# Average pooling over 64 x 256 rows: the store of a run issued by a landing signal, and one run summed by tensor_reduce

## The chip, the core and the metric

The kernel runs on one core of a Trainium2 chip. The time is device microseconds of that core for one execution, and less is better. A core has several engines that run their own instruction streams and meet through semaphores; here SyncE (SP) issues loads, VectorE (DVE) adds, ScalarE (ACT) multiplies and issues stores. All transfers are carried out by the same 16 DMA engines, whichever engine issues them. Each issuing engine has a DMA queue of its own: q1 holds what SyncE issues, q10 what ScalarE issues.

## The reference

The input is 64 x 256 x 8192 float32 numbers (537 MB). Kernel size and stride are both 4, so every output element is the mean of four neighbours that no other output uses; the output has 64 x 256 x 2048 numbers (134 MB).

```python
out_len = (length - kernel_size) // stride + 1
for i in range(out_len):
    start = i * stride
    output[:, :, i] = np.mean(x[:, :, start : start + kernel_size], axis=2)
```

## The kernel before

The input is seen as one long row and cut into 64 blocks of 128 partitions x 16384 elements (8.39 MB each, 64 KB in a partition). Two blocks make a run, so there are 32 runs, numbered 0 to 31; n is the run, k (0 or 1) the block within it. A run's output is 128 x 8192 elements (4.19 MB, 32 KB in a partition) and leaves in one store.

There are two input buffers, xt0 for the first and xt1 for the second block of every run, and two output buffers, ot0 and ot1, used in turn by even and odd runs (q in the code).

All order is written out by hand with semaphores. The helper `take` (L59) waits until a semaphore has reached a number and takes this number off again. `pair` (L82) issues the instructions of one run on all engines:

- VectorE takes `full[k]`, which block k's load counts up when it has landed; for the first block it also takes `stored[q]`, which the store out of the same output buffer, two runs earlier, counts up. Then `sums` (L74) adds neighbours: L76 adds even and odd elements into the first half of the block's own buffer, a drain follows, and L78 adds even and odd elements of that half into the output buffer.
- The end of L78 counts up `free`. SyncE takes it, counts up `summed` for ScalarE, and issues the next run's load of the same k into the buffer that came free (L63, through the argument `ahead`).
- ScalarE takes `summed` and multiplies the block's sums by a quarter in place (L94).
- After the second block, the engine given as `store` takes `scaled` and issues the run's store (L98). It is ScalarE for runs 0 to 29 and SyncE for run 30.

Runs 0 to 29 are in a loop of 15 passes with two runs each. Run 30 follows outside the loop (L123); its `ahead` loads the first block of run 31 whole and the second in two halves of columns (L114), each with a semaphore of its own. Run 31 is written out: VectorE sums the first block, then each half of the second; ScalarE multiplies, and stores in two parts (L142): 3 MB with the first half, the last 1 MB with the second. SyncE at last waits for all stores.

At the start, the loads of run 0 are issued (L70), and a small ScalarE instruction (L102) and an increment mark the two output buffers as free.

Of the kernel before, what the change touches and what calls it, by code (L numbers as in the profile page):

```python
# [1 line left out]

# [4 lines left out]


FULL = 16384
PAIR = 2  # L10
ROUND = 2 * PAIR

TAIL = (8192, 8192)


@with_exitstack
def kernel(
    ctx: ExitStack,
    tc: tile.TileContext,
    x: bass.AP,  # L20
    kernel_size: bass.AP,
    stride: bass.AP,
    out: bass.AP,
):
    nc = tc.nc
    K, S = int(kernel_size), int(stride)
    assert K == S == 4
    B, C, L = x.shape
    assert L % K == 0
    P = nc.NUM_PARTITIONS  # L30
    dt = x.dtype
    add, mult = mybir.AluOpType.add, mybir.AluOpType.mult

    M = FULL // K
    blocks = B * C * L // P // FULL
    runs = blocks // PAIR
    assert blocks * P * FULL == B * C * L and blocks % ROUND == 0 and sum(TAIL) == FULL

    xr = x.rearrange("b c l -> (b c l)").rearrange("(n p k m) -> n k p m", p=P, k=PAIR, m=FULL)
    orun = out.rearrange("b c l -> (b c l)").rearrange("(n p m) -> n p m", p=P, m=PAIR * M)  # L40


    xt0 = ctx.enter_context(nc.sbuf_tensor([P, FULL], dt))
    xt1 = ctx.enter_context(nc.sbuf_tensor([P, FULL], dt))
    ot0 = ctx.enter_context(nc.sbuf_tensor([P, PAIR * M], dt))
    ot1 = ctx.enter_context(nc.sbuf_tensor([P, PAIR * M], dt))
    xt, ot = [xt0, xt1], [ot0, ot1]


    full = [nc.alloc_semaphore(f"full{k}") for k in range(2)]  # L50
    piece = [nc.alloc_semaphore(f"piece{k}") for k in range(len(TAIL))]
    free = nc.alloc_semaphore("free")
    summed = nc.alloc_semaphore("summed")
    summed_last = nc.alloc_semaphore("summed_last")
    scaled = nc.alloc_semaphore("scaled")
    scaled_last = nc.alloc_semaphore("scaled_last")
    stored = [nc.alloc_semaphore(f"stored{k}") for k in range(2)]

    def take(engine, sem, n):  # L59
        engine.wait_ge(sem, n).then_inc(sem, -n)  # L60

    def load(n, k):
        d = nc.sync.dma_start(out=xt[k][:, :], in_=xr[n, k])  # L63
        d.then_inc(full[k], 16)
        return d

    for k in range(2):
        tc.no_tile_sem_insts.add(load(0, k).ins.name)  # L70
    tc.close()
    tc.compile()  # L72

    def sums(t, o):  # L74
        w = t.shape[1]
        nc.vector.tensor_tensor(out=t[:, : w // 2], in0=t[:, ::2], in1=t[:, 1::2], op=add)  # L76
        nc.vector.drain()
        return nc.vector.tensor_tensor(  # L78
            out=o, in0=t[:, : w // 2 : 2], in1=t[:, 1 : w // 2 : 2], op=add
        )  # L80

    def pair(n, q, ahead, store):  # L82

        for k in range(PAIR):
            take(nc.vector, full[k], 16)
            if k == 0:
                take(nc.vector, stored[q], 16)
            sums(xt[k][:, :], ot[q][:, k * M : (k + 1) * M]).then_inc(free, 1)
            take(nc.sync, free, 1)
            nc.sync.sem_inc(summed, 1)  # L90
            ahead(k)
            o = ot[q][:, k * M : (k + 1) * M]
            take(nc.scalar, summed, 1)
            means = nc.scalar.mul(o, o, 1.0 / K)  # L94
        done = scaled if store is nc.scalar else scaled_last
        means.then_inc(done, 1)
        take(store, done, 1)
        store.dma_start(out=orun[n], in_=ot[q][:, :]).then_inc(stored[q], 16)  # L98


    zero = nc.const_aps.tensor(0.0, [P, 1], dt)
    nc.scalar.mul(ot[0][:, :1], zero, 1.0).then_inc(stored[0], 16)  # L102
    nc.scalar.sem_inc(stored[1], 16)

    edges = [sum(TAIL[:i]) for i in range(len(TAIL) + 1)]
    pieces = list(zip(edges[:-1], edges[1:]))
    xe, oe = xr[runs - 1, 1], orun[runs - 1]

    def ahead_of_last(k):
        if k == 0:  # L110
            load(runs - 1, 0)
        else:
            for sem, (a, b) in zip(piece, pieces):
                nc.sync.dma_start(out=xt[1][:, a:b], in_=xe[:, a:b]).then_inc(sem, 16)  # L114

    engines = (mybir.EngineType.SP, mybir.EngineType.DVE, mybir.EngineType.Activation)
    with nc.Fori(0, (runs - 2) // 2, 1, engines=engines) as r:
        for q in range(2):
            n = r * 2 + q
            pair(n, q, lambda k: load(n + 1, k), nc.scalar)  # L120


    pair(runs - 2, 0, ahead_of_last, nc.sync)  # L123

    take(nc.vector, stored[1], 16)
    take(nc.vector, full[0], 16)
    sums(xt[0][:, :], ot[1][:, :M]).then_inc(summed_last, 1)
    for k, (sem, (a, b)) in enumerate(zip(piece, pieces)):  # L130
        take(nc.vector, sem, 16)
        sums(xt[1][:, a:b], ot[1][:, M + a // K : M + b // K]).then_inc(summed_last, 1)
        if k == 0:
            take(nc.scalar, summed_last, 1)
            nc.scalar.mul(ot[1][:, :M], ot[1][:, :M], 1.0 / K)  # L135
        o = ot[1][:, M + a // K : M + b // K]
        take(nc.scalar, summed_last, 1)
        nc.scalar.mul(o, o, 1.0 / K).then_inc(scaled, 1)  # L138
        take(nc.scalar, scaled, 1)
        c = 0 if k == 0 else M + a // K  # L140
        d = M + b // K
        nc.scalar.dma_start(out=oe[:, c:d], in_=ot[1][:, c:d]).then_inc(stored[1], 16)  # L142
    take(nc.sync, stored[0], 16)
    take(nc.sync, stored[1], 16 * len(TAIL))


# [1 line left out]
_INS = ['x', 'kernel_size', 'stride']  # L148
_OUTS = [((64, 256, 2048), 'float32')]

_NUMBERS = {'kernel_size': 4, 'stride': 4}


# [26 lines left out]
```

## Time and profile before

| | us |
|---|---|
| median of 3 runs | 1578.83 |
| lowest, highest | 1573.74, 1585.71 |
| the profiled execution, its own time | 1578.58 |
| its span in the profile | 1577.3 |
| L76 over 128 x 8192 results, mean of one | 8.692 |
| L78 over 128 x 4096 results, mean of one | 4.425 |
| L94 over 128 x 4096, mean of one | 3.616 |
| VectorE idle in front of L76, in total | 720.1 |
| ScalarE idle in front of L94, in total | 1307.6 |

The profile is of one execution. Its page lists busy time by engine and by line, the share of the span in which the 16 DMA engines moved data, in 40 equal slices and by queue, and the DMA issues with the time from issue to landing. The trace behind it answers finer questions: a timeline of instructions with the idle time before each, and busy time and bytes in any stretch. Issuing a DMA and waiting on a semaphore do not count as busy time. The trace also has a record of every packet that the DMA engines moved, with its queue, size, start and duration; a packet here is one partition's row of a block. Times in the text are microseconds from the start of the span.

### The profile page before, as it was taken

The page shows a single profiled execution, that of the slowest core. Times are in us where ns is not written, and L with a number is a line of the kernel's source. Part 1 is how long each engine was busy: PE and PEld are TensorE (multiplying, and loading weights), DVE is VectorE, ACT ScalarE, POOL GpSimd, SP SyncE. Part 2 cuts the span into 40 slices and gives each one's busy share as a digit, 9 for nine tenths or more (in the row PEclk, how much of TensorE's full clock was granted, in tenths as well). Part 3 has the DMA queues.
Part 4 walks back from the last instruction along what each step waited for, and adds up shares of the span by engine and source line. Part 5 has one row for each costly group of instructions (what it writes and reads, how often), then busy time and mean ns, then how long its engine had stood idle before and what let it go on. Part 6 is the DMA issues. An engine that isn't in the chain of part 4 may idle for free. (4 is left out here: it accounts for less than half of the span.)

```text
span 1577.3 us, 1028 instructions
## 1 busy us (share of the span) xinstructions
DVE 839.8 (53%) x130; ACT 233.1 (15%) x67; POOL 0.2 (0%) x4
## 2 busy tenths in 40 slices
DVE  3654546545465454654546545465454654546546
ACT  1101011010110101101011010110101101011011
POOL 0000000000000000000000000000000000000000
DMA  9999999999999999999999999999999999999999
GB/s 425 425 425 425 435 439 420 430 434 430 420 427 419 445 420 427 420 420 444 425 425 412 425 438 424 422 415 425 437 425 427 414 421 441 417 430 420 416 435 388
DMA packets 14112, 671.09 MB, mean 425 GB/s; under 512 B 1568, under 2 KB 1568, under 8 KB 1568
## 3 DMA queue, kind: packets, MB, share of 16 engines
q1 hardware_dynamic: 9504, 541.07, 80.7%
q10 hardware_dynamic: 4608, 130.03, 19.1%
HBM read 536.87 MB, written 134.22 MB: 425 GB/s over the span
## 5 line engine op out<-in xcount | busy, mean ns | idle before, releaser
L76 DVE TENSOR_TENSOR xt<-xt 128x8192 f32<-128x8192 f32 (+1 forms) x65 | 556.5, 8561 | 720.1 <-DVEq L60 720.1
L94 ACT ACTIVATE ot<-ot 128x4096 f32<-128x4096 f32 x62 | 224.2, 3616 | 1307.6 <-ACTq L60 1307.6
L78 DVE TENSOR_TENSOR ot<-xt 128x4096 f32<-128x4096 f32 (+1 forms) x65 | 283.4, 4360 | 4.8
L135 ACT ACTIVATE ot<-ot 128x4096 f32<-128x4096 f32 x1 | 3.6, 3617 | 15.6 <-ACTq L60 15.6
L138 ACT ACTIVATE ot<-ot 128x2048 f32<-128x2048 f32 x2 | 3.8, 1910 | 8.0 <-ACTq L60 8.0
L102 ACT ACT_TABLE_LOAD x1 | 1.3, 1283 | 2.4 <-PEq L72 2.4
L102 ACT ACTIVATE ot<-const-float32-0.0 128x1 f32<-128x1 f32 x1 | 0.2, 203 | 0.0
L161 POOL MEMSET const-bfloat16-1.0<- 128x1 bf16 x1 | 0.1, 102 | 0.0
L161 POOL MEMSET const-uint8-127<- 128x1 uint8 x1 | 0.1, 102 | 0.0
L161 POOL MEMSET const-float32-1.0<- 128x1 f32 x1 | 0.1, 99 | 0.0
L161 POOL MEMSET const-float32-0.0<- 128x1 f32 x1 | 0.1, 98 | 0.2 <-issue 0.2
## 6 DMA issues: line engine op xcount, KB each, us to landing
out_dram<-ot ACTq DMA_DIRECT2D x30, 4096.0 KB, 33.8
xt<-in_x_dram SPq DMA_DIRECT2D x2, 4096.0 KB, 20.5
out_dram<-ot SPq DMA_DIRECT2D x1, 4096.0 KB, 34.4
out_dram<-ot ACTq DMA_DIRECT2D x1, 3072.0 KB, 13.8
out_dram<-ot ACTq DMA_DIRECT2D x1, 1024.0 KB, 10.4
xt<-in_x_dram SPq DMA_DIRECT2D x63, 35.6
```

The lines of the kernel that those rows point to most:

```text
L76: nc.vector.tensor_tensor(out=t[:, : w // 2], in0=t[:, ::2], in1=t[:, 1::2], op=add)
L78: return nc.vector.tensor_tensor(out=o, in0=t[:, : w // 2 : 2], in1=t[:, 1 : w // 2 : 2], op=add)
L94: means = nc.scalar.mul(o, o, 1.0 / K)
L102: nc.scalar.mul(ot[0][:, :1], zero, 1.0).then_inc(stored[0], 16)
L135: nc.scalar.mul(ot[1][:, :M], ot[1][:, :M], 1.0 / K)
L138: nc.scalar.mul(o, o, 1.0 / K).then_inc(scaled, 1)
L161: nc = _bacc.Bacc("TRN2", target_bir_lowering=False, num_devices=1)
```

## The change

ScalarE's store gets one more wait. A new semaphore, `landed`, is counted up by VectorE whenever it has taken `full[0]`, that is, when the first block of a run has landed, before it begins its sums. ScalarE takes one count of it ahead of issuing a run's store. Since run 0's own first block also counts it up, ScalarE takes one count at the start, so that the store of run n waits for the first block of run n + 1. This holds for runs 0 to 29. The store of run 30, which SyncE issues, and those of run 31 don't wait for it.

In run 30, both blocks are summed by a new function, `reduce`: one `tensor_reduce` over groups of four neighbours, from the input buffer to the output buffer, in place of the two additions and the drain. All other runs keep `sums`.

```diff
+    landed = nc.alloc_semaphore("landed")
...
+    def reduce(t, o):
+        return nc.vector.tensor_reduce(
+            out=o,
+            in_=t.rearrange("p (m k) -> p m k", k=K),
+            op=add,
+            axis=mybir.AxisListType.X,
+        )
+
     def pair(n, q, ahead, store):
         for k in range(PAIR):
             take(nc.vector, full[k], 16)
             if k == 0:
+                nc.vector.sem_inc(landed, 1)
                 take(nc.vector, stored[q], 16)
-            sums(xt[k][:, :], ot[q][:, k * M : (k + 1) * M]).then_inc(free, 1)
+            add_up = sums if store is nc.scalar else reduce
+            add_up(xt[k][:, :], ot[q][:, k * M : (k + 1) * M]).then_inc(free, 1)
...
         means.then_inc(done, 1)
         take(store, done, 1)
+        if store is nc.scalar:
+            take(store, landed, 1)
         store.dma_start(out=orun[n], in_=ot[q][:, :]).then_inc(stored[q], 16)
...
     nc.scalar.sem_inc(stored[1], 16)
+    take(nc.scalar, landed, 1)
```

## The prediction, made before the change was built

> **What bounds the kernel now.** I read the page first for who is full, then the timeline of one run of the steady loop, then the page's list of DMA issues and a table of short windows.
>
> The page, engine shares, the row of DMA tenths, and the queues (packets, MB, share of the 16 DMA engines' span):
>
> ```profile
> DVE 839.8 (53%) x130; ACT 233.1 (15%) x67; POOL 0.2 (0%) x4
> ...
> DMA  9999999999999999999999999999999999999999
> ...
> q1 hardware_dynamic: 9504, 541.07, 80.7%
> q10 hardware_dynamic: 4608, 130.03, 19.1%
> HBM read 536.87 MB, written 134.22 MB: 425 GB/s over the span
> ```
>
> The two queues together fill 99.8% of the DMA engines' time; VectorE is half idle, ScalarE mostly idle. The bytes are fixed by the reference. So the change can win only what the DMA engines lose inside their busy time, and can lose only by leaving them without work.
>
> The timeline, steady state and end (start, duration, engine, line; in brackets the idle time before):
>
> ```profile
> 1437.63 0.34 ACTq L98 DMA_DIRECT2D out_dram<-ot  x1
> 1439.83 8.69 DVE L76 TENSOR_TENSOR xt<-xt 128x8192 f32<-128x8192 f32 x1 [6.27 <-DVEq L60]
> ...
> 1469.62 8.69 DVE L76 TENSOR_TENSOR xt<-xt 128x8192 f32<-128x8192 f32 x1 [16.60 <-DVEq L60]
> 1478.39 4.43 DVE L78 TENSOR_TENSOR ot<-xt 128x4096 f32<-128x4096 f32 x1
> 1483.03 3.62 ACT L94 ACTIVATE ot<-ot 128x4096 f32<-128x4096 f32 x1 [26.18 <-ACTq L60]
> 1486.89 0.34 ACTq L98 DMA_DIRECT2D out_dram<-ot  x1
> 1489.08 8.69 DVE L76 TENSOR_TENSOR xt<-xt 128x8192 f32<-128x8192 f32 x1 [6.26 <-DVEq L60]
> ...
> 1518.67 8.69 DVE L76 TENSOR_TENSOR xt<-xt 128x8192 f32<-128x8192 f32 x1 [16.40 <-DVEq L60]
> ...
> 1532.02 0.81 SPq L114 DMA_DIRECT2D xt<-in_x_dram  x2
> ...
> 1535.79 0.34 SPq L98 DMA_DIRECT2D out_dram<-ot  x1
> 1538.02 8.69 DVE L76 TENSOR_TENSOR xt<-xt 128x8192 f32<-128x8192 f32 x1 [6.16 <-DVEq L60]
> ...
> 1566.85 0.35 ACTq L142 DMA_DIRECT2D out_dram<-ot  x1
> ```
>
> Every L76 instruction starts when its block has landed. From a run's first block (1439.83) to its second (1469.62) are 29.79 us; from there to the next run's first (1489.08) 19.46; together 49.25. A block is 128 rows, 8 on each DMA engine (14,112 packets over 98 DMAs and 16 engines are 9: eight rows and a small one). The 19.46 us are a load alone, 2.42 us a row of 64 KB. The 29.79 us hold another load and the whole store, whose 8 rows of 32 KB alternate with the load's. The reader should also see that the store is issued 2.19 us before the next run's first block is taken (1486.89, 1489.08), and why: both count from the landing of the second block, the store at 8.69 + 4.43 + 3.62 us and three handovers, the block at eight rows.
>
> The same view near the start:
>
> ```profile
> 61.53 8.69 DVE L76 TENSOR_TENSOR xt<-xt 128x8192 f32<-128x8192 f32 x1 [6.27 <-DVEq L60]
> ...
> 107.50 0.34 ACTq L98 DMA_DIRECT2D out_dram<-ot  x1
> 110.94 8.69 DVE L76 TENSOR_TENSOR xt<-xt 128x8192 f32<-128x8192 f32 x1 [7.52 <-DVEq L60]
> ...
> 159.27 8.69 DVE L76 TENSOR_TENSOR xt<-xt 128x8192 f32<-128x8192 f32 x1 [6.24 <-DVEq L60]
> ```
>
> From 61.53 to 1489.08 are 29 periods, 49.23 us each. One of them, 110.94 to 159.27, took 48.33: exactly 16 load rows of 2.42 and 8 store rows of 1.21. So the engines lose 0.9 us in a usual period, some 26 us in all, and this is all that an order of stores could win. Where it is lost the packet records of the trace show: load rows take 2.42 us, but for one or two on each engine about the time that a store begins, which take 2.5 to 3.7. A table of windows (DVE, ACT, POOL busy, clock, DMA share, GB/s) shows the dip behind the store of 1437.63:
>
> ```profile
> 1437.60:1447.60 10.00, 7.77 (x1) 0.00 (x0) 0.00 (x0) 1.00 0.98 387
> 1447.60:1457.60 10.00, 5.34 (x2) 3.62 (x1) 0.00 (x0) 1.00 1.00 433
> ```
>
> **The change part by part.**
>
> 1. *The wait in front of the store.* The signal is given when VectorE takes the next run's first block, just before L76 starts. ScalarE's own handover, from the end of L94 (1483.03 + 3.62) to the issue at 1486.89, took 0.24 us; with that for the new one, the issue moves from 1486.89 to about 1489.3, 2.4 us later. That is almost exactly one load row (2.42). In the packet records the slowest engine ends its eighth row 0.6 us before VectorE starts, so 1.6 us after the issue now and 0.8 us before it then; modulo one row the store meets the loads in the same phase. Hence I take the loss at a store's start as it is, 0.9 us a run: cost 0. Its bounds: nothing (48.33 us a period, minus 26 us in all) and the longest period in the trace, 49.66 (plus 0.43 x 30 = plus 13 us). The trace of before has no store issued at this place, so both ends stay in the range.
>
> 2. *What is queued behind the waiting store.* On ScalarE: the next run's L94, which needs sums that end 13.2 us after the same landing; ScalarE has been idle 15.8 and 26 us before each L94. On the DMA engines: no load waits, since loads are issued by SyncE when a block's sums are done, not by the store. While the store waits, the second block's load, issued 13.2 us after the previous landing, keeps the engines full. Who waits for the store: VectorE, before it writes the same output buffer again, one whole period after the new issue (49.2 us).
>
> ```profile
> out_dram<-ot ACTq DMA_DIRECT2D x30, 4096.0 KB, 33.8
> ```
>
> It lands 33.8 us (median) after its issue, so 15 us are left, against 17.6 now. Cost 0; if that cover were gone, VectorE would stand still, and it has 6.3 us to spare even then.
>
> 3. *Where the moved row goes.* One store row of 1.21 us goes out behind the second block rather than before it. So the second block lands 1.2 us sooner after the first (about 28.6) and the first one 1.2 us later (20.7). The sum of a period stays.
>
> 4. *The extra instructions.* One semaphore increment on VectorE and one wait on ScalarE a run, well under 0.1 us beside 6 us of idle time; and a wait at the start on ScalarE, which idles 32 us there. Cost 0.
>
> 5. *tensor_reduce in run 30, both blocks.* Two additions of 8.69 and 4.43 us and the drain, 13.20 us together, become one instruction over 16,384 inputs. The trace has no reduction. L76 makes one result per 1.061 ns from two inputs; one input per step gives 16,384 x 1.061 = 17.4 us, two inputs per step 8.7. Upper bound: two steps an input, 34.8. I take 17.4, plus 4.2 a block. The Trainium skill speaks against it (VectorE: DVE Perf Modes, Rules for kernel authors): a reduction is to be expected at the plain rate, and it calls this the slowest operation of the engine; at the clock that its Specifications give, an estimate is 17.1 us, and the sum would be the same.
>    The first reduction delays the load of the last run's first block from 1502.5 to 1506.7, while the load before it runs until 1517: hidden. The second delays the last two loads (L114, 1532.02). They must be ready when the block taken at 1538.02 has been transferred, by 1537.4 on the slowest engine. Now they are issued 5.4 us ahead of this; then 5.4 - 4.2 = 1.2 us, or 2.4 with the 1.2 us of step 3. The first load of all had data 1.0 us after its issue (packet records). So 0 to 1 us is lost; I take 0.5. SyncE's store of run 30 (1535.79) moves by 3 us, but is queued behind 19 us of loads on its own queue: 0. VectorE, done at about 1535, still waits for the block of 1538: 0.
>
> Sum: +0.5 us on the profiled execution's 1578.58 (span 1577.3), which lies 0.25 us under the median of 1578.83. **Forecast 1579 us**, no change. By the spread of the runs shown (1573.74 to 1585.71) and a loss at the store's start between 0.6 and 1.1 us, its own range is 1570 to 1588.
>
> **The rivals.**
>
> - *The store's start loses nothing any more* (faster). For: the one period with no loss in which the store had been issued 3.44 us ahead of the landing shows that the loss depends on where a store falls. Against: there every engine was in step, and in the new place the phase is that of the usual ones. All gone gives 1579 - 26 = 1553; half gone 1566.
> - *The store's start loses more* (slower, mostly within 1%). The engines stand up to 3.5 us apart at the landing; the second block's load is issued 4 us before the store now and 8 us before it then, so faster engines may run further ahead, and the store meets them more scattered. Runs with longer periods are those of the later half, when the engines have drifted apart. At 49.66 a period 1592; over 1% from 49.75 on; at double the loss 1605.
> - *The reduction becomes the bound* (slower). Its place is the end alone. From about 18.5 us a reduction on, the last loads come after the engines have run dry, and each further us costs a us. At 34.8 us VectorE would take the second block of run 30 at 1524 and finish at 1559, so the last loads start 27 us later than 1532, less the 3 us to spare: 1602. For: the row is a two-input instruction, which tells nothing certain of another kind. Against: nothing says that an input takes two steps.
> - *The change does not do what it says*: if the block had landed before ScalarE's multiplication was done, the wait would be met at once and the time the same. The rows exclude it (2.19 us, 3.44 at most), but the delay is 5% of a period, so little differs.
>
> **How the numbers follow.** Forecast 0.66 (with the fourth rival), store's start cheaper 0.14, dearer 0.13, reduction 0.07. About 1%, 15.8 us, is what a measurement of this kernel can tell from no change. The forecast lies within it; of the cheaper case 0.12 goes beyond, of the dearer 0.09, of the reduction 0.06. Faster 0.12, same 0.73, slower 0.15. The range for 8 in 10 reaches from half of the loss gone, 1565, to the longest period and a bit more, 1594.
>
> **What would show it.** Right: DMA tenths all 9 and 425 GB/s; the store of ScalarE some 0.2 us behind the first L76 of a run, no longer 2.19 ahead; VectorE's idle times near 15.4 and 7.5 us in place of 16.6 and 6.3; a period of 49.0 to 49.4; a reduction of 17 us and the last two loads issued at 1535. Wrong: periods near 48.4 (first rival) or over 49.7 (second); a reduction over 18.5 us with a slice of DMA below 9 before the end (third); a VectorE wait ended by a store's landing, which step 2 excludes.

## The result and the profile after

The changed kernel takes 1569.93 us (median of 16 runs, 1560.34 to 1572.9) beside 1577.17 us for the kernel before (16 runs in the same sessions). The ratio is 0.9942, with a 95% interval of 0.992 to 0.9965: by this ratio 9 us less, clear of no change (the two medians lie 7 us apart). The profiled execution took 1570.50 us, with a span of 1569.2.

The page of the changed kernel, with the same lines as of before (engine shares, DMA tenths, the two queues with packets, MB and share, the sum) and the store's row of the DMA issues:

```profile
DVE 848.0 (54%) x128; ACT 233.1 (15%) x67; POOL 0.2 (0%) x4
...
DMA  9999999999999999999999999999999999999999
...
q1 hardware_dynamic: 9504, 541.07, 80.6%
q10 hardware_dynamic: 4608, 130.03, 19.2%
HBM read 536.87 MB, written 134.22 MB: 428 GB/s over the span
...
out_dram<-ot ACTq DMA_DIRECT2D x30, 4096.0 KB, 33.4
```

The same bytes take the same share of the engines' time, 99.8%, in a span 8.1 us shorter. What became less is time lost inside the engines' busy time; the page alone can't show it.

The timeline of the changed kernel, steady state and end (L77 and L84 are the first instruction of a block, L112 the store; start, duration, engine, line, and in brackets the idle time before):

```profile
1431.01 8.69 DVE L77 TENSOR_TENSOR xt<-xt 128x8192 f32<-128x8192 f32 x1 [7.54 <-DVEq L61]
1431.05 0.34 ACTq L112 DMA_DIRECT2D out_dram<-ot  x1
...
1459.15 8.69 DVE L77 TENSOR_TENSOR xt<-xt 128x8192 f32<-128x8192 f32 x1 [14.95 <-DVEq L61]
...
1479.88 17.22 DVE L84 TENSOR_REDUCE ot<-xt 128x4096 f32<-128x16384 f32 x1 [7.54 <-DVEq L61]
1479.92 0.34 ACTq L112 DMA_DIRECT2D out_dram<-ot  x1
...
1507.90 17.22 DVE L84 TENSOR_REDUCE ot<-xt 128x4096 f32<-128x16384 f32 x1 [10.80 <-DVEq L61]
1525.28 0.82 SPq L129 DMA_DIRECT2D xt<-in_x_dram  x2
...
1528.42 8.69 DVE L77 TENSOR_TENSOR xt<-xt 128x8192 f32<-128x8192 f32 x1 [3.31 <-DVEq L61]
1529.05 0.34 SPq L112 DMA_DIRECT2D out_dram<-ot  x1
...
1549.84 4.43 DVE L77 TENSOR_TENSOR xt<-xt 128x4096 f32<-128x4096 f32 x1 [1.52 <-DVEq L61]
...
1558.78 0.35 ACTq L157 DMA_DIRECT2D out_dram<-ot  x1
```

The store (1431.05) now comes 0.04 us behind the first block's first addition (1431.01); before, it came 2.19 us ahead. From first to second block are 28.14 us here (29.79 before), from there to the next first block 20.73 (19.46). Over the 29 periods from the second run's first block (61.54) to 1479.88 the mean is 48.91 us, beside 49.23: 9.2 us gained. From run 30's first block to the end of the span are 89.3 us, beside 88.2: 1.1 us given back.

In the table below, "store" is the store's issue in the steady state, counted from the first addition of the next run's first block; "lead" is the time from the issue of the second block's load to that same point, in all but two kernels read as VectorE's idle time in front of it, which is 0.3 us more than the time from the issue itself; "end" runs from run 30's first block to the end of the span. Store, lead, period and end come from the one profiled execution of each kernel; ratios are of the times, to the kernel before on the same chip.

| kernel | store us | lead us | period us | end us | ratio (95% interval) |
|---|---|---|---|---|---|
| before | -2.2 | 6.3 | 49.23 | 88.2 | 1 |
| the change | 0.0 | 7.5 | 48.91 | 89.3 | 0.9942 (0.9920 to 0.9965) |
| e1, wait only | 0.0 | 7.5 | 48.96 | 87.5 | 0.9921 (0.9891 to 0.9951) |
| e2, reduction only | -2.2 | 6.3 | 49.19 | 89.9 | 1.0005 (0.9977 to 1.0032) |
| e3, wait, late load | 0.6 | 3.5 | 49.98 | 88.8 | 1.0149 (1.0115 to 1.0182) |
| e4, four-step sums, two multiplications | 0.9 | 6.9 | 48.39 | 87.1 | 0.9842 (0.9808 to 0.9877) |
| e5, early load, early store | -7.7 | 11.8 | 48.37 | 85.7 | 0.9828 (0.9781 to 0.9876) |
| e6, early load, store's old place | -2.7 | 10.5 | 48.37 | 87.0 | 0.9826 (0.9779 to 0.9873) |
| e7, late load, later store | 9.0 | 8.2 | 48.45 | 87.0 | 0.9838 (0.9791 to 0.9885) |
| e8, later store | 9.0 | 12.2 | 48.38 | 87.0 | 0.9827 (0.9780 to 0.9874) |
| e9, short lead | 9.0 | 4.6 | 48.61 | 87.1 | 0.9955 (0.9924 to 0.9987) |
| e10, middle lead | 9.0 | 8.4 | 48.45 | 87.0 | 0.9856 (0.9833 to 0.9879) |
| e11, wait, early load | 0.0 | 11.8 | 48.78 | 89.8 | 0.9919 (0.9880 to 0.9959) |
| e12, two halvings | 0.3 | 7.5 | 48.87 | 88.2 | 0.9955 (0.9920 to 0.9991) |
| e13, store 3.8 us on | 3.8 | 9.9 | 48.40 | 86.9 | 0.9840 (0.9791 to 0.9890) |

In e9 and e10, SyncE holds the load back; there the lead is VectorE's idle time (12.2) less 7.6 and 3.8 us. e4, e5, e6 and e11 leave out a quarter of the second block's elements in the loop runs, and so do not compute the reference; they serve to time the loads.

### The profile page after: what moved, and what is told of

Same layout as the page of the kernel before. It is cut to its first block, busy times and chain, and to the rows that moved or that the text cites. A ratio compares the mean times of both kernels' runs of the same rounds, so it can differ in the third digit from the quotient of the medians.

```text
span 1569.2 us, 1086 instructions
## 1 busy us (share of the span) xinstructions
DVE 848.0 (54%) x128; ACT 233.1 (15%) x67; POOL 0.2 (0%) x4
## 5 line engine op out<-in xcount | busy, mean ns | idle before, releaser
L77 DVE TENSOR_TENSOR xt<-xt 128x8192 f32<-128x8192 f32 (+1 forms) x63 | 539.1, 8557 | 685.6 <-DVEq L61 685.6
L79 DVE TENSOR_TENSOR ot<-xt 128x4096 f32<-128x4096 f32 (+1 forms) x63 | 274.5, 4358 | 4.7
L84 DVE TENSOR_REDUCE ot<-xt 128x4096 f32<-128x16384 f32 x2 | 34.4, 17220 | 18.3 <-DVEq L61 18.3
## 6 DMA issues: line engine op xcount, KB each, us to landing
out_dram<-ot ACTq DMA_DIRECT2D x30, 4096.0 KB, 33.4
```

Source lines behind the costliest of these rows:

```text
L79: return nc.vector.tensor_tensor(out=o, in0=t[:, : w // 2 : 2], in1=t[:, 1 : w // 2 : 2], op=add)
L84: return nc.vector.tensor_reduce(out=o, in_=t.rearrange("p (m k) -> p m k", k=K), op=add, axis=mybir.AxisListType.X,)
```

## The two halves of the change

The first two runs part the wait from the reduction.

e1, the wait alone:

```diff
-            add_up = sums if store is nc.scalar else reduce
+            add_up = sums
```

> Only the wait in front of the store; run 30 keeps its two additions. The whole change took 9.2 us off the 29 steady periods (49.23 to 48.91 us each) and lost 1.1 us behind the first block of run 30 (88.2 us before, 89.3 after). If the wait makes the first and the reduction the second, this kernel has periods of about 48.9 and 88.2 us of end: 9 us less than before, ratio 0.994, 1 us less than the whole change. If the reduction had a part in the gain, it is not below the whole change.

e2, the reduction alone: the change without its three `landed` edits.

> Only the reduction in run 30, no wait in front of the store. Expected by both theories: periods as before, 49.2 us, and an end about 1 us longer, ratio 1.000 to 1.001.

The wait alone gives 0.9921, the reduction alone 1.0005. So the whole gain is the wait's. The reduction costs something at the end, too little for these intervals to show; the profiled executions, one of each kernel, show it: 89.9 us beside 88.2 without the wait, 89.3 beside 87.5 with it, 1.7 to 1.8 us either way. (Drift between the engines lengthens the end too: e11, without a reduction but with the engines 8.7 us apart, has 89.8.) Where it goes can be seen in the DMA view of 10 us around the last loads (queue, packets, MB, share of the engines' time). Before, 1532 to 1542, the loads' queue alone fills the engines; in the changed kernel, 1522 to 1532, it leaves 21% of the ten us empty.

```profile
q1 hardware_dynamic: 129, 4.23, 98.0%
```

```profile
q1 hardware_dynamic: 104, 3.18, 79.0%
```

The second reduction ends at 1525.12, the loads are issued at 1525.28, and by the packet records their first rows start 1.0 to 1.5 us later; fifteen engines had finished the load before between 1523.6 and 1525.2 and stood empty until then, so that the sixteen lost 2.0 us each on average. VectorE, too, then waits 1.52 us for the second piece (1549.84), which it did not before.

## Which cause: the place of the store, its distance from the load, or the load's lead

The packet records of both kernels raise the question. A record does not name its DMA engine; the rows were put to engines by their times, since on one engine a row starts where the one before it ends. In the kernel before, the load rows stretched about a store's start cost an engine 0.55 us a run in runs 1 to 10 and 0.92 in runs 11 to 29. In the changed kernel it is 0.03 in runs 1 to 10 and 0.64 later. In the early runs hardly more than one engine loses anything, about 0.25 us a run; it falls behind, until the other fifteen finish the first block's load 2 to 5 us ahead of it, and the first of them is there some 2 us after the second block's load has been issued (6.6 us after it, the slowest).

Two theories were set against each other first. The **lead**: an engine loses when the next load was issued shortly before it needs its rows. The **place**: what counts is where the store starts between the two loads. e3 shortens the lead and keeps the place; e4 was meant to lengthen the lead and keep the place of before.

e3:

```diff
-            add_up = sums if store is nc.scalar else reduce
+            add_up = reduce if k == 1 and store is nc.scalar else sums
```

> The wait as in the change, but the second block of every loop run is summed by a reduction (17.2 us in place of 13.2), run 30 by two additions. So the next run's second load is issued 4 us later: some 3.3 us ahead of the store, as in the kernel before (3.8), in place of 7.3; the store keeps its new place behind the landing. Theory of the load: the loss at a store's start comes when the second block's load is issued so late that the fastest engines reach the end of the first block about when the new rows become ready; it is back here, periods 49.2 us or more, ratio 1.000 or over. Theory of the place: what counts is that the store starts after all engines have passed from the first block's load to the second's; then periods stay at 48.9 and the ratio at 0.994.

e4, from the kernel before:

```diff
+    def three(t, o):
+        nc.vector.tensor_tensor(out=o, in0=t[:, ::K], in1=t[:, 1::K], op=add)
+        nc.vector.drain()
+        return nc.vector.tensor_tensor(out=o, in0=o, in1=t[:, 2::K], op=add)
...
-            sums(xt[k][:, :], ot[q][:, k * M : (k + 1) * M]).then_inc(free, 1)
+            short = k == 1 and store is nc.scalar
+            add_up = three if short else sums
+            add_up(xt[k][:, :], ot[q][:, k * M : (k + 1) * M]).then_inc(free, 1)
...
+            if short:
+                nc.scalar.mul(o, o, 1.0)
+                nc.scalar.drain()
             means = nc.scalar.mul(o, o, 1.0 / K)
```

> The kernel before, without the wait, but the second block of the loop runs leaves out the fourth of every four elements: two additions of 4096 results, about 8.9 us in place of 13.2, so that the next run's second load is issued about 4.3 us earlier. ScalarE multiplies that block twice (once by 1) so that the store keeps its old place, about 2.2 us ahead of the landing. Theory of the load: the loss goes although the store has not moved, periods about 48.5, 20 us less in all, ratio 0.986 to 0.992. Theory of the place: periods stay at 49.2, ratio 1.000.

The timeline of e3, one period:

```profile
1061.97 8.69 DVE L77 TENSOR_TENSOR xt<-xt 128x8192 f32<-128x8192 f32 x1 [3.51 <-DVEq L61]
1062.62 0.34 ACTq L112 DMA_DIRECT2D out_dram<-ot  x1
...
1111.92 8.69 DVE L77 TENSOR_TENSOR xt<-xt 128x8192 f32<-128x8192 f32 x1 [3.52 <-DVEq L61]
```

49.95 us for this period, and 1.0149 in all: with 3.5 us of lead more is lost than the wait wins. That the loss comes from the lead alone is not shown by this run, as rows that come late also leave engines empty.

The timeline of e4:

```profile
933.00 8.69 DVE L76 TENSOR_TENSOR xt<-xt 128x8192 f32<-128x8192 f32 x1 [6.92 <-DVEq L60]
933.84 0.34 ACTq L108 DMA_DIRECT2D out_dram<-ot  x1
...
981.32 8.69 DVE L76 TENSOR_TENSOR xt<-xt 128x8192 f32<-128x8192 f32 x1 [6.76 <-DVEq L60]
```

e4 gained 25 us, but not as planned. Its two additions with a step of four took 7.4 us each, so the load came later, not earlier (a lead of 6.9 us, a little under the change's 7.5), and the two multiplications pushed the store to 0.84 us behind the first addition. It has almost the change's place and lead, and yet periods of 48.3 us with no loss. Something of some tenths of a us decides.

The second set therefore also tests a third theory, the **distance** in time between the load's issue and the store's. e5 and e6 use sums with a step of two for the second block; e6 is e5 with e4's second multiplication. e8 gives the signal behind the first addition instead of ahead of it; e7 does the same to e3.

```diff
+    def three(t, o):
+        h = FULL // 2
+        nc.vector.tensor_tensor(out=o, in0=t[:, :h:2], in1=t[:, 1:h:2], op=add)
+        nc.vector.drain()
+        return nc.vector.tensor_tensor(out=o, in0=o, in1=t[:, h::2], op=add)
```

> The kernel before, without the wait. The second block of the loop runs gets two additions of 4096 results with steps of two (8.9 us in place of 13.2): three elements in four are added, and not the ones of the reference. The load of the next second block is then issued 4.3 us earlier, and so is the store, which stays 3.8 us behind that load and comes 6.5 us ahead of the landing. Theory of the load's lead (the loss comes when the load is issued shortly before the fastest engines need its rows): no loss, periods 48.4 to 48.6, ratio 0.984 to 0.989. Theory of the distance (the loss comes when a store is issued within about 4 us behind a load, and is gone at 7 us): periods stay at 49.2, ratio 1.000.

> As the one with the early store, but ScalarE multiplies that block twice, so that the store goes back to its old place, about 2.5 us ahead of the landing, now 7.5 us behind the load. This is what the kernel with the four-step additions was meant to be (those took 7.4 us each, so its load came later, not earlier, and its store 2 us behind the landing). Both the theory of the lead and that of the distance: no loss, 48.4 to 48.6 a period, ratio 0.984 to 0.989. The theory of the place (a store must start behind the landing): periods of 49.2, ratio 1.000.

e8, from e1; in e7 the second block of the loop runs keeps e3's reduction and all others get these sums:

```diff
-    def sums(t, o):
+    def sums(t, o, tell=False):
...
         nc.vector.drain()
+        if tell:
+            nc.vector.sem_inc(landed, 1)
...
-                nc.vector.sem_inc(landed, 1)
...
-            add_up = sums
-            add_up(xt[k][:, :], ot[q][:, k * M : (k + 1) * M]).then_inc(free, 1)
+            sums(xt[k][:, :], ot[q][:, k * M : (k + 1) * M], k == 0).then_inc(free, 1)
```

> The kernel with the wait and the late load (second block of the loop runs by a reduction; 1.015 with the store 3.9 us behind the load), but VectorE counts up the signal behind the first of the two additions of the first block, 8.8 us later: the store is then about 12.6 us behind the load, whose lead is as short as there. Theory of the lead: the loss stays, ratio 1.010 to 1.020. Theory of the distance: the loss goes, periods fall from 50 to about 49, ratio 0.990 to 1.000; what is left is engines that wait for rows.

> The wait alone, with the signal given 8.8 us later (behind the first addition of the next run's first block): the store is 16 us behind the load, the load's lead as with the wait alone. Theory of the lead: about as the wait alone, periods 48.8 to 48.9, ratio 0.992 to 0.994. Theory of the distance: the loss that the wait alone still has is gone too, periods 48.4 to 48.6, ratio 0.984 to 0.989.

All four run at 48.4 to 48.5 us a period. The timeline of e5:

```profile
927.11 0.34 ACTq L106 DMA_DIRECT2D out_dram<-ot  x1
934.82 8.69 DVE L76 TENSOR_TENSOR xt<-xt 128x8192 f32<-128x8192 f32 x1 [11.78 <-DVEq L60]
...
983.17 8.69 DVE L76 TENSOR_TENSOR xt<-xt 128x8192 f32<-128x8192 f32 x1 [11.80 <-DVEq L60]
```

The theory of the distance falls with e5: its store comes 3.8 us behind its load, as in the kernel before, and nothing is lost. Nor does a store need to come behind the landing: e5's comes 7.7 us ahead of it, e6's 2.7. The timeline of e6:

```profile
1075.02 0.34 ACTq L109 DMA_DIRECT2D out_dram<-ot  x1
1077.74 8.69 DVE L76 TENSOR_TENSOR xt<-xt 128x8192 f32<-128x8192 f32 x1 [10.48 <-DVEq L60]
...
1126.10 8.69 DVE L76 TENSOR_TENSOR xt<-xt 128x8192 f32<-128x8192 f32 x1 [10.51 <-DVEq L60]
```

e6 is the run that speaks for the lead. Its store stays within 0.6 us of its old place, its load has 4.2 us more lead than in the kernel before (10.5 and 6.3), and the loss is gone.

The timeline of e8:

```profile
1077.67 8.69 DVE L77 TENSOR_TENSOR xt<-xt 128x8192 f32<-128x8192 f32 x1 [12.20 <-DVEq L61]
1086.63 0.34 ACTq L112 DMA_DIRECT2D out_dram<-ot  x1
...
1126.03 8.69 DVE L77 TENSOR_TENSOR xt<-xt 128x8192 f32<-128x8192 f32 x1 [12.12 <-DVEq L61]
```

e8 computes the whole reference with no more work than the kernel before, and it takes 1553.03 us: it beats both. But it does not part lead from place, nor does e7. With the store issued later, more of its rows go out between a run's second block and the next run's first, which therefore lands later (25.4 us behind the second block in e8, 19.5 in the kernel before). The second block's load, issued when the sums are done, then has more lead: 12.2 us in e8, and in e7 8.2, not the 3.5 of e3 as its expectation assumed.

## Place and lead apart

The third set holds the place far out and shortens the lead (e9, e10, both from e8), lengthens the lead at the change's own place (e11, e1 with e5's sums), and moves the store by work instead of by a signal (e12, from the kernel before).

e9 (in e10, SyncE takes a count that the first halving gives):

```diff
+    halved = nc.alloc_semaphore("halved")
...
-            ahead(k)
+            held = k == 1 and store is nc.scalar
+            if not held:
+                ahead(k)
...
-            means = nc.scalar.mul(o, o, 1.0 / K)
+            if held:
+                nc.scalar.mul(o, o, 0.5)
+                nc.scalar.drain()
+                means = nc.scalar.mul(o, o, 0.5)
+                take(nc.sync, halved, 1)
+                ahead(k)
+            else:
+                means = nc.scalar.mul(o, o, 1.0 / K)
...
         if store is nc.scalar:
+            store.sem_inc(halved, 1)
             take(store, landed, 1)
```

> The kernel with the later store (0.983, no loss; store 21 us behind the load, that load issued 12 us before the landing of the block ahead of it), but SyncE holds the next run's second load of the loop runs back until ScalarE has multiplied twice by a half: about 7.6 us later. The load is then issued some 4.6 us ahead of that landing (6.3 in the kernel before, 3.5 in the one with the late load), the store still 13 us behind it. Theory of the lead: the loss is back, periods 49.0 to 50.0, ratio 0.996 to 1.015. Theory of the distance between load and store: no loss, periods about 48.4, ratio 0.983.

> The same, held back until the first of the two multiplications only: about 3.8 us later, 8.4 us ahead of the landing. Both theories: no loss, ratio 0.983; a loss here would put the point of the theory of the lead above 8 us.

> The wait alone at the place of the change, with the short sums of the second block (two additions of 4.4 us, three elements in four added, and not the ones of the reference), so that the second load is issued 4.3 us earlier, about 11.8 us ahead of the landing in place of 7.5; the store keeps its place behind the landing. Theory of the lead: the loss that the change leaves (48.9 a period) goes, 48.4 a period, ratio 0.983. If the place of the store itself costs something, it stays at 0.990 to 0.994.

e12:

```diff
-            means = nc.scalar.mul(o, o, 1.0 / K)
+            if k == 1 and store is nc.scalar:
+                nc.scalar.mul(o, o, 0.5)
+                nc.scalar.drain()
+                means = nc.scalar.mul(o, o, 0.5)
+            else:
+                means = nc.scalar.mul(o, o, 1.0 / K)
```

> The kernel before, with neither wait nor reduction; ScalarE multiplies the second block of the loop runs twice by a half, so that the store comes 3.8 us later by work instead of by a signal: about 0.5 us behind the landing, 7.5 us behind the load. If the gain of the change comes from the later store and not from the signal, this gains as much: ratio 0.990 to 0.995. By the theory of the lead not more, since the load is issued as in the change.

e12 comes to 0.9955 without any signal: what the change wins is the later store, however it is brought about. Its timeline shows the place, 0.31 us behind:

```profile
1087.76 8.69 DVE L76 TENSOR_TENSOR xt<-xt 128x8192 f32<-128x8192 f32 x1 [7.44 <-DVEq L60]
1088.07 0.34 ACTq L103 DMA_DIRECT2D out_dram<-ot  x1
```

e11 contradicts the lead as the cause of what the change leaves: with 11.8 us of lead the ratio stays at 0.9919.

```profile
1085.77 8.69 DVE L77 TENSOR_TENSOR xt<-xt 128x8192 f32<-128x8192 f32 x1 [11.79 <-DVEq L61]
1085.81 0.34 ACTq L119 DMA_DIRECT2D out_dram<-ot  x1
...
1134.63 8.69 DVE L77 TENSOR_TENSOR xt<-xt 128x8192 f32<-128x8192 f32 x1 [11.81 <-DVEq L61]
```

Its packet records are the clearest of all. In runs 1 to 20 the slowest engine loses 0.39 us a run and the other fifteen 0.03 to 0.05; the period is 48.7 us, for the slowest engine sets it. The fifteen get ahead by that much every run, until in runs 21 to 29 the load is issued, on their average, only 2.6 to 3.1 us before they need it. Then they lose 0.46 us a run, and the slowest 0.55. So there are two losses, and the first leads to the second.

e9 stays half open. Its ratio, 0.9955, says that a short lead costs 20 us beside e8 even with the store far out, and e10 with a middle lead shows none of that (0.9856). But its runs lie between 1558.91 and 1581.3 us, and the profiled one, 1559.70, was among the fastest: behind run 2, it has periods of 48.3 to 48.4 us (48.7 the last) with next to no loss. Where its longer executions lose time was not seen.

The packet records of all the kernels together, one entry for each engine and each of the runs 1 to 29 (6,960), sorted by when the store was issued, counted from the moment at which the engine itself had passed from the first block's load to the second's, and by how long before this moment the second load had been issued. The entries are us lost to stretched rows, those that start between 3 us before the earlier and 8 us behind the later of passing and issue:

```
load issued        store issued, us behind the engine's passing
us before          -9 to -2   -2 to 1.5   1.5 to 6   over 6
4.5 or more          0.00        0.22       0.01      0.00
2.5 to 4.5            -          0.75       0.34      0.04
under 2.5             -          0.96       1.10      0.89
```

With 4.5 us of lead or more, hardly any engine loses unless the store is issued from 2 us before to 1.5 us behind its own passing. In the changed kernel the store is issued 0.7 us behind the slowest engine's passing, inside the window, and 1.6 us or more behind that of the others (but for one in the first runs), outside; in the kernel before, the engines pass from 2.0 us before to 1.9 us behind the store's issue from run 2 on, three quarters of them inside; in e4, which began this, from 1.4 to 2.4 us before it, nearly all of them just outside.

Not every engine inside the window loses, though, and e6 shows where. Its store is issued 1.1 to 2.0 us before the passing in 432 of 464 entries, and nothing is lost; in the kernel before and in e2, engines at 1.2 to 1.75 us with at least 4.5 us of lead lose 0.60 us. Their loads had been issued 5.0 to 5.5 us before the passing, e6's 8.6 to 9.6. So a store just ahead of the passing is harmless when the load has lead enough, or something that goes with it; no run parts the two. Behind the passing this does not help: e11's slowest engine has 10.8 us of lead and loses. Without e6, the 0.22 of the table is 0.43.

This makes a forecast of its own: move the change's store by some 4 us, and the loss should be gone, with no need of e8's 9 us. One more run tried it.

e13, from e1; ScalarE does the second half of its multiplication behind the wait:

```diff
-            means = nc.scalar.mul(o, o, 1.0 / K)
+            held = k == 1 and store is nc.scalar
+            means = nc.scalar.mul(o, o, 0.5 if held else 1.0 / K)
+        if store is nc.scalar:
+            take(nc.scalar, landed, 1)
+            nc.scalar.drain()
+            means = nc.scalar.mul(o, o, 0.5)
...
-        if store is nc.scalar:
-            take(store, landed, 1)
```

> The wait alone, but ScalarE multiplies the second block by a half before the wait and by a half again behind it, so that the store is issued about 3.8 us behind the landing in place of 0.05. By the packet records of the runs so far an engine loses nothing when the store comes 1.5 us or more behind its passing, if its rows were issued early enough. Theory of the place: all engines are past the window, they stay together, periods 48.4, ratio 0.983 to 0.986. If only the lead counts (the load is issued as in the change, 7.5 us ahead of the landing, one store row more), or if the later store needed its whole 8.8 us, the ratio stays at 0.990 to 0.994.

```profile
1078.29 3.62 ACT L111 ACTIVATE ot<-ot 128x4096 f32<-128x4096 f32 x1 [5.99 <-ACTq L61]
1078.33 8.69 DVE L77 TENSOR_TENSOR xt<-xt 128x8192 f32<-128x8192 f32 x1 [9.87 <-DVEq L61]
1082.14 0.34 ACTq L115 DMA_DIRECT2D out_dram<-ot  x1
...
1126.70 8.69 DVE L77 TENSOR_TENSOR xt<-xt 128x8192 f32<-128x8192 f32 x1 [9.82 <-DVEq L61]
```

0.9840, 48.37 us for this period: the whole loss is gone. The lead has grown with the later store, to 9.9 us from the change's 7.5, but it is not what decides here: e11 has 11.8 us at the change's place and loses, e4 has 6.9 us with the store 0.9 us later and does not. So behind the landing the store's place decides, and the window's far edge lies between 0.3 us (e12) and 0.9 us (e4) behind the first addition. With the store outside, the engines stay closer together (0.6 us apart in e13's early runs, 1.7 at its end; 4.5 in the change), and no lead runs out.

## Why the prediction was wrong

The forecast was no change, 1579 us; measured were 9 us less, just under the 1570 to 1588 that the forecast gave itself. The wide range, 1565 to 1594, holds the 1569.93, and the case that happened stands among the rivals, but it was not the one chosen.

- **What bounds the kernel** was right: the DMA engines are at 99.8% after as before, and the only thing to win was the 0.9 us at a store's start. The floor taken from one period, 48.33 us, is real: e5 holds 48.35 for the period shown and 48.37 in the mean.
- **Step 1 failed.** It took the loss to depend on where the store meets a row: "modulo one row the store meets the loads in the same phase. Hence I take the loss at a store's start as it is". The place came out as worked out, 0.04 us behind the first addition where 0.2 was said, so about one row later, and the loss still fell from 0.86 to 0.54 us a period (49.23 and 48.91 over the floor of 48.37). What counts there is not the phase in a row but the distance to the engine's own passing from one load to the next, and one row more was enough to bring all but the slowest engine, and early on one other, out of that window. (Ahead of the passing the lead counts as well, as e6 shows.) The period without loss, 110.94 to 159.27, pointed there: its store came 3.44 us ahead of the landing instead of 2.19, and the packet records put every engine's passing 2.2 to 2.9 us behind the store, outside the window on the near side. The prediction put it down to engines in step.
- **The first rival** had the right mechanism and a third of its size: 9.2 us of the 26. The rest is what the slowest engine still loses, and what the others lose once they are too far ahead; e8 and e13 win it too.
- **The second rival** said that the faster engines would run further ahead. They do: by 4.5 us in runs 11 to 29 of the change, 3.4 before (the load is issued 7.2 us ahead of the store, where 8 was said). It costs only when their next load comes too late, and the balance was a gain.
- **Steps 2 to 4** held: VectorE waits for no store, the store takes 33.4 us to land, a run's second block lands 28.2 us behind the first and the next first block 20.7 (28.6 and 20.7 were said; the second block's time also has the loss in it).
- **Step 5** had the reduction's length right: 17.22 us measured, 17.4 said. The plain rate that the Trainium skill states (VectorE: DVE Perf Modes, Rules for kernel authors), with the clock of its Specifications an estimate of 17.1 us, agrees. The cost of the reduction was mis-sized: 0.5 us was taken and 0 to 1 the bounds; e1 and e2 put it at 1.7 to 1.8. The step counted from the slowest engine, which needs the last loads at 1537.5 in the kernel before; the packet records have the other fifteen ready for them from 1534.4 to 1535.6, and those are the ones that ran dry.
- **The third rival** let the engines run dry from a reduction of 18.5 us on, counted from the slowest engine too. Fifteen of them ran dry at 17.22 us, for 2.1 us on average; as the bound of the whole kernel the reduction did not come up.

Why an engine loses time when a second queue starts while it goes from one load to the next, or when that load is only just there, no run shows. The packet records show it as load rows of 2.5 to 3.8 us, rarely up to 4.3, in place of 2.42, just in front of an engine's first store row or between its first and second, and no more.

## What to carry to other kernels

In a kernel that is bound by its DMA engines, it is worth asking at which point of the load stream the stores start: here a store moved by 6 us against the kernel before (e13), with the same bytes and queues, was worth 1.6%, and the first try, moved by 2.2 us, reached a third of it. An earlier load won as much with the store close to its old place (e6). Look for the fastest period in the trace before taking a DMA share of 99.8% as the end; where one period is faster than the mean, something in the others may be lost. And issue a load well before the first engine needs it, not the last: the engines drift apart when one of them loses a little every round, and the fast ones then find the next load not ready.

## What was not expected of the hardware

The 16 DMA engines drift apart over a kernel. In the kernel before, their ends of one load were 0.7 us apart in the second run and 3.4 us later; with no loss at a store's start (e8) they were 0.4 us apart in the second run and 1.2 at the end. One engine was behind the others in nearly every run.

A VectorE addition with a step of four elements took 7.4 us for 4096 float32 results (e4), one with a step of two 4.43 (e5): 1.81 and 1.08 ns a result. The Trainium skill (SBUF — State Buffer, Door 1: The DMA port swizzle) describes lines of 16 bytes in the memory that need two hits each for the full rate, and says that float32 can be strided by up to four for free. With a step of two a line gets two hits, with a step of four one: the first statement agrees with both durations, the second does not with the 7.4 us, and the measurement decides. Why a step of four costs this much was not tested further.
